# A hybrid decoder layer on one core: two products taken in turn, a DMA turn in the attention, and three shifts of order

## The chip, the core and the metric

The kernel runs on one core of a Trainium2 chip. Its engines work side by side, each through its own queue in order: TensorE (PE, whose weight loads are listed as PEld), VectorE (DVE), ScalarE (ACT), GpSimd (POOL), and SyncE (SP), which here only issues DMAs. The metric is the device time of one execution in microseconds (us); smaller is better. Three executions of the kernel before took 2025.03 us in the median (2021.9 to 2025.69).

## What is computed

One decoder layer for 256 tokens of width 2048, in float32. Cut to what the change touches:

```python
hn = rmsnorm(h, norm_mix_w)
q, k, v, g_ret, xr, yr, g_a, g_b = split(hn @ w_in)
ret = head_groupnorm(chunkwise_retention(rotary(q), rotary(k), v), ret_gn_w)
ret_out = silu(g_ret) * ret
rnn_out = gelu(yr) * rg_lru(causal_dwconv(xr))
merged = sigmoid(g_a) * (ret_out @ w_proj_ret) + sigmoid(g_b) * (rnn_out @ w_proj_rnn)
h = h + merged @ w_mix_out
...
logits = einsum("bshd,bmhd->bhsm", q, k) * 512 ** -0.5     # 4 heads, 256 memory tokens
p = softmax(logits)
o = einsum("bhsm,bmhd->bshd", p, v)
h = h + o @ xa_w_o
h = h + conv_gated_ffn(rmsnorm(h, norm_ffn_w))
return rmsnorm(h, final_norm_w)
```

## The kernel before

**Products.** All weights are laid out in DRAM in the order in which they are used (`weight_stream`, L110), in chunks of four k-tiles: 512 rows by 512 columns of float32, 1 MB. A product of 256 tokens with a 2048 x 512 block of weights is four chunks. To reach nearly float32 accuracy, both operands are split into a high part and a rest, and three matmuls replace one (`products_n`, L340: high x high, low x high, high x low). A chunk is so 24 matmuls of 128 x 128 by 512.

**Supply of weights.** `prefetch` (L228) issues a chunk's load on SP's queue into one of 3 `raw` buffers; ScalarE copies it to `hi` (L269) and VectorE subtracts to get `lo` (L270), each for two k-tiles at a time, into 6 buffers of two k-tiles, which is three chunks. `chunks` (L284) runs the prefetch two chunks ahead of the chunk that is multiplied. A `raw` buffer is free for the next load when its `lo` is done; a `hi` or `lo` buffer when TensorE has used it.

**Work between chunks.** After each chunk a counter goes up by one; `later(n, fn)` (L280) emits `fn` after n + 1 further chunks. The order of the matmuls on TensorE is the order in which they are written. On the other engines a planner orders the instructions: of those that it takes to be ready, the one that was written first goes first, apart from a few with high priority (the copies of `by_dma`, the scaling in `turned_rows`).

**Turning.** A product gives rows by token; the next one needs them by feature. `by_dma` (L372) does it: ScalarE copies the 16-bit halves of the rows to two `planes` (L380), SP issues two transposing DMAs (L382), and after `wait` + 1 chunks two ScalarE copies (L391) join the halves to `f`. `split_pair` (L416) or `split_cols` (L442) then makes the high and low operands.

**Around the change.** `retain` (L603) runs four heads of the retention at a time; after the last head `normalise` (L640) scales the eight half-rows of the four heads by VectorE (L648) and ScalarE (L653) and turns them in two pieces; the results, `words`, are first used some 60 chunks later. `gated` (L799) makes a block of the merge; block 3 of `merged` is the last thing before the product with `w_mix_out`, whose chunk k needs block k of `merged`. `residual` (L828) runs the four blocks of that product and, later, of the one with `xa_w_o`: each block's sum is added to the residual rows (L835), squared (L850), and turned. `memory_steps` (L854) adds, ahead of block 1, eight squarings of the memory's rows (L488). The eight 512 KB loads of x and of the memory (L824 and L825) stand on SP's queue just ahead of that product. In the cross attention a product for k and one for q alternate for four heads; `softmax` (L874) makes the probabilities, `transpose_probs` (L896) turns them by four TensorE transposes (L209) and a ScalarE copy (L906); `attend` (L925) multiplies them with v, one chunk after v's product.

At the start two products run in turn already, in chunks of 2, 2, 4, 4 and 4 k-tiles, fed by loads of x by feature (`xt`, L525). The rows of x by token (`nat`, L223) are only needed for the sum of squares that scales the first results; their four loads are issued on ScalarE's queue.

Of the kernel before, what the change touches and what calls it, by code (L numbers as in the profile page):

```python
# [106 lines left out]
    return [(sum(sizes[:j]), n) for j, n in enumerate(sizes)]  # L107


def weight_stream():  # L110

    out = [
        [(w, row + k * P, n, c) for k, n in pieces(i, nk)]
        for i, (w, row, nk, c) in enumerate(weight_plan())
    ]
    out[:2] = [[one for pair in zip(*out[:2]) for one in pair]]
    out[-4:-1] = [[c for o in out[-4:-1] for c in o[:-1]] + [o[-1] for o in out[-4:-1]]]
    return [one for chunks in out for one in chunks]


# [10 lines left out]
def hybrid_layer(  # L131
# [73 lines left out]
    def mm(*a, **k):  # L205
        tc.keep_in_program_order(pe.matmul(*a, **k))  # L206

    def turn_small(*a):
        tc.keep_in_program_order(pe.transpose(*a))  # L209


    plan = weight_plan()
    stream = weight_stream()
# [4 lines left out]
    def load_x(n):  # L218
        while len(xin) < n:
            t = big([P, 2, BW], s="nat")  # L220
            rows = x[0].rearrange("(t p) d -> p t d", p=P)
            c = len(xin) * BW
            act.dma_start(out=t, in_=rows[:, :, c : c + BW])  # L223
            xin.append(t)

    at = [0]
# [1 line left out]
    def prefetch(n):  # L228
        while len(ahead) < n and taken[0] < len(stream):
            i = taken[0]  # L230
            name, row, nk, c = stream[i]
            taken[0] += 1
            size = nk * P * BW
            src = wall[at[0] : at[0] + size].rearrange("(p k n) -> p k n", p=P, k=nk)
            at[0] += size
            raw = wp.tile([P, KC, BW], F32, tag="raw", bufs=RAW_BUFS, name=nm("raw"))
            k2 = row // (KH * P)
            early = i < 2 * len(EARLY)
            own = early and i % 2 == 0
            cuts = range(nk + 1) if i < 2 else range(0, nk + 1, KH) if i < 6 else (0, nk)  # L240
            if own:
                xs.load(k2 + 1)
            for a, b in zip(cuts, cuts[1:]):
                sp.dma_start(out=raw[:, a:b, :], in_=src[:, a:b, :])  # L244
                if i == 0 and a == 0:
                    sp.dma_start(out=xs.rest[0], in_=xs.rest[1])
                elif own and a == 0:
                    xs.load(k2 + nk // KH)
            if i == 7:
                sp.dma_start(out=cid, in_=consts[:, 0:C_DEC])  # L250
                sp.dma_start(out=pa[:, 16:P], in_=by_feature[:, 16:P])
                sp.dma_start(out=pb, in_=by_feature[:, P : P + 80])
            if i == 11:
                sp.dma_start(out=pf.rearrange("p a n -> p (a n)"), in_=by_feature[:, P + 80 :])
            if i in (8, 9):
                for b in (2 * i - 16, 2 * i - 15):
                    sum_squares(xin[b], ss0, b, pin=True)
            parts = []
            for k in range(0, nk, KH):
                if own:  # L260
                    xs[k2 + k // KH]
                hi = wp.tile([P, KH, BW], F32R, tag="hi", bufs=PART_BUFS, name=nm("hi"))
                lo = wp.tile([P, KH, BW], F32R, tag="lo", bufs=PART_BUFS, name=nm("lo"))
                for cs in (slice(k, k + 1), slice(k + 1, k + 2)) if i < 2 else (slice(k, k + KH),):
                    ds = slice(cs.start - k, cs.stop - k)
                    if i == 0:
                        dve.tensor_copy(hi[:, ds], raw[:, cs, :])  # L267
                    else:
                        act.copy(hi[:, ds], raw[:, cs, :])  # L269
                    dve.tensor_tensor(  # L270
                        out=lo[:, ds], in0=raw[:, cs, :], in1=hi[:, ds].bitcast(F32), op=ALU.subtract
                    )
                parts.append((hi, lo))
            ahead.append(((row, c), parts))
            if i >= 4:
                load_x(min(4, i - 3))

    pending, step = [], [0]

# [323 lines left out]
    def retain(g, qr, kr, vs, dec, gates):  # L603
# [34 lines left out]
                normalise()  # L638

        def normalise():  # L640
            rows = [big([P, 2, BW], s="rows") for _ in range(2)]
            rstd = rsqrt_small(stats[:, :, 1], 8, 1.0, GN_EPS).rearrange("p (h t) -> p h t", t=2)
            for tt in range(2):
                dve.tensor_scalar_mul(rstd[:, :, tt], rstd[:, :, tt], rs0[:, tt : tt + 1])
            for hh in range(4):
                for tt in range(2):
                    y = raws[hh][:, tt, :]
                    dve.scalar_tensor_tensor(  # L648
                        out=y, in0=y, scalar=stats[:, 2 * hh + tt, 0:1],
                        in1=gates[hh // 2][:, tt, (hh % 2) * DV : (hh % 2 + 1) * DV],  # L650
                        op0=ALU.subtract, op1=ALU.mult,
                    )
                    act.mul(rows[hh // 2][:, tt, (hh % 2) * DV : (hh % 2 + 1) * DV], y, rstd[:, hh, tt : tt + 1])  # L653
            for i, r in enumerate(rows):
                by_dma(r, words.append, 2 + i)

        for hh in range(4):
            later(hh, lambda hh=hh: scores(hh))
# [159 lines left out]
    for b in range(4):  # L818
        m = gated(O_GA, "w_proj_ret", ret, b, big([P, 2, BW], s="m"))
        dve.tensor_add(m, m, mb[b])  # L820
        by_dma(m, turn_merged)


    hrow = [load_rows(x, c) for c in range(4)]  # L824
# [3 lines left out]
    def residual(w, st, out, wcol, steps=None):  # L828

        ss = sums()  # L830
        for b in range(4):
            if steps:
                steps(b)
            h = hrow[b]
            dve.tensor_add(h, h, gemm_n(w, 0, st, NT, b * BW))  # L835
            squares(h, ss, b)
            by_dma(hrow[b], lambda f, b=b: turn(f, b, out, wcol))
        return ss
# [30 lines left out]
    lscale = sp_.tile([P, 2], F32, tag="ls", name="lscale")  # L869
    dve.tensor_scalar_mul(lscale, rstd_rows(ss1), float(XD**-0.5))  # L870

    pTs, done = [], [0]

    def softmax(q, k):  # L874
        lg = small()
        for tt in range(2):
            for i in range(4):
# [4 lines left out]
        mx, nb, sm, rsm = (sp_.tile([P, 2], F32, tag=f"sx{i}", name=nm("sx")) for i in range(4))  # L882
        dve.tensor_reduce(out=mx, in_=lg, axis=AX.X, op=ALU.max)
        dve.scalar_tensor_tensor(out=nb, in0=mx, scalar=-1.0, in1=lscale, op0=ALU.mult, op1=ALU.mult)
        pr_ = tmp("prob")
        for tt in range(2):
            c1 = slice(tt, tt + 1)
            act.activation(
# [2 lines left out]
        dve.reciprocal(rsm, sm)  # L891
        for tt in range(2):
            dve.tensor_scalar_mul(pr_[:, tt, :], pr_[:, tt, :], rsm[:, tt : tt + 1])
        later(1, lambda: transpose_probs(pr_))

    def transpose_probs(pr_):  # L896
        t = small()
        for kt in range(2):
            for tt in range(2):
                turn_small(t[:, kt, tt * P : (tt + 1) * P], pr_[:, tt, kt * P : (kt + 1) * P], ident)  # L900
        if done[0] == len(pTs):
            two = tp.tile([P, 2, BW], F32, tag="sig", bufs=2, name=nm("pT"))
            pTs.extend(two[:, i, :].rearrange("p (k s) -> p k s", s=S) for i in range(2))
        pT = pTs[done[0]]
        done[0] += 1
        act.copy(pT, t)  # L906

    def split_block(f):
        return [split_pair(f[:, 2 * pr : 2 * pr + 2, :]) for pr in range(2)]
# [1 line left out]
    def key_query(b):  # L911
# [2 lines left out]

        def query(f):
            qs = split_block(f)
            later(1, lambda: softmax(qs, ks))

        turned_rows(gemm_n("xa_w_q", 0, h1s, NT, b * BW), None, query)

# [19 lines left out]

    for b in range(XH):
        v = split_rows(gemm_n("xa_w_v", 0, ms, NT, b * BW), rsms[0])
        later(0, lambda b=b, v=v: attend(b, v))

    h2s = []
    ss2 = residual("xa_w_o", osp, h2s, p_ffn)
# [153 lines left out]
```

## Time and profile before

| what | before |
|---|---|
| median of the runs (lowest, highest) | 2025.03 us (2021.9, 2025.69) |
| the profiled execution: time, and span from its first to its last instruction | 2022.28 us, 2020.5 us |
| mean granted TensorE clock | 0.996 |
| VectorE busy, ScalarE busy | 1264.3 us, 1246.0 us |
| DMA: moved, mean rate | 421.99 MB, 209 GB/s |

How to read the lines further down: in a chain of waits or a timeline the first number is the start in us from the first instruction, the second the time taken; `x24` counts instructions that were merged into one row; `[4.04 <-ACT s L423]` says that the engine idled 4.04 us before and what ended it. In groups of instructions, `busy, mean ns` is followed by the idle time ahead of the group's instructions. In a table of windows each engine has its busy us and the number of instructions that touch the window; then follow the granted clock, the DMA engines' busy share and the rate.

### The profile page before, as it was taken

What the parts mean: (1) busy time and instruction counts of PE and PEld (TensorE: products, weight loads), DVE (VectorE), ACT (ScalarE), POOL (GpSimd) and SP (SyncE); (2) the same over time, 40 slices, a digit from 0 to 9 for tenths busy, and PEclk for the clock granted to TensorE, in tenths of its full rate; (3) what the DMA queues carried; (4) which work ended last, traced back from release to release, by engine and by line L of the source; (5) the groups of instructions that cost most, each with busy time, mean ns of one, the idle gap of its engine ahead of it and who ended that gap; (6) DMA issues with size and microseconds to landing.
All of it is one profiled execution on the core that took longest, in us unless ns stands there. A gap on an engine that the chain in (4) does not pass through costs nothing.

```text
span 2020.5 us, 23630 instructions
## 1 busy us (share of the span) xinstructions
PE 2002.3 (99%) x9060; PEld 1666.2 (82%) x9060; DVE 1264.3 (63%) x1563; ACT 1246.0 (62%) x1502; POOL 7.7 (0%) x12
## 2 busy tenths in 40 slices
PE   9999999999999999999999999999999999999998
PEld 7888888888888888788888888888888888888887
DVE  5856756888645555456555554567675577664675
ACT  6546547989434555478666556666774566644763
POOL 0000000000000000000000000000000000000000
PEclk9999999999999999999999999999999999999999
DMA  8665656665555566777766546667666566655663
GB/s 304 225 210 173 234 199 192 228 213 188 208 188 190 197 204 214 259 225 242 219 198 204 182 167 208 209 189 218 228 203 232 193 195 214 227 215 198 210 228 125
DMA packets 185153, 421.99 MB, mean 209 GB/s; under 512 B 127440, under 2 KB 132176, under 8 KB 139984
## 3 DMA queue, kind: packets, MB, share of 16 engines
q1 hardware_dynamic: 183520, 417.85, 62.2%
q10 hardware_dynamic: 1520, 2.63, 0.4%
q8 instruction: 71, 1.16, 0.2%
q14 instruction: 42, 0.34, 0.1%
HBM read 388.46 MB, written 2.10 MB: 193 GB/s over the span
## 4 chain that ended last, share of the span: by engine, by line
PE 97%; ACT 1%; DVE 1%; DMA 1%; issue 1%; SPq 0%; POOL 0%; POOLq 0%; DVEq 0%; ACTq 0%
PE acc L206 94%; PE sm L206 3%; DMA raw<-in_wall 1%; DVE lo L270 0%; ACT f L391 0%; DVE xr L765 0%; ACT pl L380 0%; ACT rows L653 0%; ACT hi L269 0%; POOL ro L507 0%; PE sm L209 0%; SPq L244 0%; DVE s L447 0%; ACT nat L1034 0%; DVE rows L404 0%
## 5 line engine op out<-in xcount | busy, mean ns | idle before, releaser
L206 PE MATMUL acc<-hi,s 128*128 128x512 f32 (+1 forms) x5680 | 1741.6, 388 | 4.2 <-ACT s L423 4.0
L270 DVE TENSOR_TENSOR lo<-raw,hi 128x1024 fp32r<-128x1024 f32 (+1 forms) x714 | 861.1, 1220 | 662.4 <-ACT hi L269 636.5
L206 PEld LDWEIGHTS acc<-hi,s 128*128 128x128 f32 x5680 | 1062.5, 188 | 222.1 <-ACT s L423 4.5
L206 PE MATMUL acc<-lo,s 128*128 128x512 f32 (+1 forms) x2840 | 1100.8, 388 | 2.0 <-DVE lo L270 2.0
L269 ACT CAST hi<-raw 128x1024 fp32r<-128x1024 f32 (+1 forms) x712 | 736.0, 1051 | 535.4 <-PE acc L206 466.7
L206 PEld LDWEIGHTS acc<-lo,s 128*128 128x128 f32 x2840 | 533.7, 188 | 111.6 <-DVE lo L270 2.7
L391 ACT COPY f<-pt 128x1024 uint16<-128x1024 uint16 x114 | 146.5, 1350 | 68.8 <-DMA pt<-pl 68.6
L380 ACT COPY pl<-rows 128x1024 uint16<-128x1024 uint16 x90 | 89.8, 1046 | 66.1 <-DVE rows L404 58.2
L404 DVE TENSOR_SCALAR rows<-acc,ro 128x512 f32<-128x512 f32 x68 | 47.8, 747 | 2.4 <-PE acc L206 2.4
L957 DVE SCALAR_TENSOR_TENSOR fv<-f,pf,fv 128x255 f32<-128x255 f32 (+1 forms) x88 | 35.8, 479 | 0.7 <-ACT fv L955 0.7
L957 DVE SCALAR_TENSOR_TENSOR fg<-f,pf,fg 128x255 f32<-128x255 f32 (+1 forms) x88 | 35.6, 478 | 0.0
L955 ACT ACTIVATE fv<-f,pf 128x256 f32<-128x256 f32 x44 | 22.9, 596 | 0.0
L955 ACT ACTIVATE fg<-f,pf 128x256 f32<-128x256 f32 x44 | 22.9, 594 | 0.0
L423 ACT ACTIVATE s<-fo 128x512 fp32r<-128x512 f32 x22 | 13.6, 635 | 14.1 <-DVE fo L977 14.1
L380 ACT COPY pl<-nat 128x1024 uint16<-128x1024 uint16 x16 | 16.0, 1046 | 9.6 <-DVE nat L835 9.6
L765 DVE SCALAR_TENSOR_TENSOR xr<-f,pa,xr 128x255 f32<-128x255 f32 (+2 forms) x48 | 20.1, 481 | 2.1 <-ACT xr L763 2.0
L446 ACT ACTIVATE s<-f,pb 128x256 fp32r<-128x256 f32 x48 | 20.4, 501 | 0.0
L447 DVE SCALAR_TENSOR_TENSOR s<-f,pb,s 128x256 fp32r<-128x256 f32 x48 | 19.9, 480 | 0.0
L206 PEld LDWEIGHTS sm<-s,s 128*128 128x128 f32 x144 | 18.8, 191 | 0.9
L206 PE MATMUL acc<-s,hi 128*128 128x512 f32 x64 | 17.6, 413 | 1.0 <-DVE hi L267 1.0
L206 PE MATMUL sm<-s,s 128*128 128x256 f32 (+1 forms) x144 | 18.6, 279 | 0.0
L421 DVE TENSOR_TENSOR s<-f,s 128x512 fp32r<-128x512 f32 x16 | 10.3, 687 | 10.0 <-ACT s L420 10.0
(154 smaller groups left out, 630.0 us busy)
## 6 DMA issues: line engine op xcount, KB each, us to landing
raw<-in_wall SPq DMA_DIRECT2D x352, 1024.0 KB, 4.9
raw<-in_wall SPq DMA_DIRECT2D x6, 512.0 KB, 6.4
nat<-in_x ACTq DMA_DIRECT2D x4, 512.0 KB, 8.2
nat<-in_x SPq DMA_DIRECT2D x4, 512.0 KB, 5.7
nat<-in_mem SPq DMA_DIRECT2D x4, 512.0 KB, 9.0
xt<-in_mem_t SPq DMA_DIRECT2D x8, 256.0 KB, 3.7
pt<-pl SPq DMA_TRANSPOSE x114, 4.9
xt<-in_x_t SPq DMA_DIRECT2D x7, 256.0 KB, 6.3
```

Source lines behind the costliest of these rows:

```text
L206: tc.keep_in_program_order(pe.matmul(*a, **k))
L269: act.copy(hi[:, ds], raw[:, cs, :])
L270: dve.tensor_tensor(out=lo[:, ds], in0=raw[:, cs, :], in1=hi[:, ds].bitcast(F32), op=ALU.subtract)
L380: act.copy(planes[:, :, h, :], words[:, h])
L391: act.copy(halves_[:, h], turned_[:, h])
L404: dve.tensor_scalar_mul(rows[:, tt, :], a[:, tt, :], r[:, tt : tt + 1])
L423: act.mul(t[:, :, 0:S], src, scale)
L446: act.activation(t[:, j, 0:S], src[:, j, :], AF.Identity, scale=wcol(j))
L447: dve.scalar_tensor_tensor(out=t[:, j, S:BW], in0=src[:, j, :], scalar=wcol(j), in1=t[:, j, 0:S].bitcast(F32), op0=ALU.mult, op1=ALU.subtract,
L765: dve.scalar_tensor_tensor(out=y[:, s:S], in0=z[:, 0 : S - s], scalar=p_cw(3 - s, t), in1=y[:, s:S], op0=ALU.mult, op1=ALU.add,)
L955: act.activation(y, z[:, j, :], AF.Identity, scale=pf[:, 2, t : t + 1], bias=pf[:, 3, t : t + 1])
L957: dve.scalar_tensor_tensor(out=y[:, s:S], in0=z[:, j, 0 : S - s], scalar=pf[:, 2 - s, t : t + 1], in1=y[:, s:S], op0=ALU.mult, op1=ALU.add,)
```

## The change

- `weight_stream` lays the first two blocks of `w_mix_out`, and the first two of `xa_w_o`, in turn: three chunks of block 0, three of block 1, then the last chunk of each. `residual` runs the matmuls in that order. The last block of `merged` is joined at wait 3 in place of 1.
- `softmax` writes the probabilities of two heads into one `big` tile, which `by_dma` turns; the four TensorE transposes per head and the copy out of PSUM are gone. `attend` runs two chunks after v's product in place of one.
- In `normalise` the scaling by ScalarE and the turn are emitted one chunk later for heads 0 and 1 and two chunks later for heads 2 and 3; their join comes at wait 4 in place of 2 and 3.
- The loads of x by token move from ScalarE's queue to SP's, one prefetch step later and ahead of that step's copies. Three loads of constants move from step 7 to 8, one from 11 to 13.

```diff
--- before.py
+++ after.py
@@ -107,6 +107,11 @@
     return [(sum(sizes[:j]), n) for j, n in enumerate(sizes)]
 
 
+def in_turn(products):
+
+    return [c for o in products for c in o[:-1]] + [o[-1] for o in products]
+
+
 def weight_stream():
 
     out = [
@@ -114,7 +119,10 @@
         for i, (w, row, nk, c) in enumerate(weight_plan())
     ]
     out[:2] = [[one for pair in zip(*out[:2]) for one in pair]]
-    out[-4:-1] = [[c for o in out[-4:-1] for c in o[:-1]] + [o[-1] for o in out[-4:-1]]]
+    out[-4:-1] = [in_turn(out[-4:-1])]
+    for w in ("w_mix_out", "xa_w_o"):
+        i = [c[0][0] for c in out].index(w)
+        out[i : i + 2] = [in_turn(out[i : i + 2])]
     return [one for chunks in out for one in chunks]
 
 
@@ -205,9 +213,6 @@
     def mm(*a, **k):
         tc.keep_in_program_order(pe.matmul(*a, **k))
 
-    def turn_small(*a):
-        tc.keep_in_program_order(pe.transpose(*a))
-
 
     plan = weight_plan()
     stream = weight_stream()
@@ -220,7 +225,7 @@
             t = big([P, 2, BW], s="nat")
             rows = x[0].rearrange("(t p) d -> p t d", p=P)
             c = len(xin) * BW
-            act.dma_start(out=t, in_=rows[:, :, c : c + BW])
+            sp.dma_start(out=t, in_=rows[:, :, c : c + BW])
             xin.append(t)
 
     at = [0]
@@ -246,11 +251,13 @@
                     sp.dma_start(out=xs.rest[0], in_=xs.rest[1])
                 elif own and a == 0:
                     xs.load(k2 + nk // KH)
-            if i == 7:
+            if i >= 5:
+                load_x(min(4, i - 4))
+            if i == 8:
                 sp.dma_start(out=cid, in_=consts[:, 0:C_DEC])
                 sp.dma_start(out=pa[:, 16:P], in_=by_feature[:, 16:P])
                 sp.dma_start(out=pb, in_=by_feature[:, P : P + 80])
-            if i == 11:
+            if i == 13:
                 sp.dma_start(out=pf.rearrange("p a n -> p (a n)"), in_=by_feature[:, P + 80 :])
             if i in (8, 9):
                 for b in (2 * i - 16, 2 * i - 15):
@@ -272,8 +279,6 @@
                     )
                 parts.append((hi, lo))
             ahead.append(((row, c), parts))
-            if i >= 4:
-                load_x(min(4, i - 3))
 
     pending, step = [], [0]
 
@@ -638,7 +643,6 @@
                 normalise()
 
         def normalise():
-            rows = [big([P, 2, BW], s="rows") for _ in range(2)]
             rstd = rsqrt_small(stats[:, :, 1], 8, 1.0, GN_EPS).rearrange("p (h t) -> p h t", t=2)
             for tt in range(2):
                 dve.tensor_scalar_mul(rstd[:, :, tt], rstd[:, :, tt], rs0[:, tt : tt + 1])
@@ -650,9 +654,17 @@
                         in1=gates[hh // 2][:, tt, (hh % 2) * DV : (hh % 2 + 1) * DV],
                         op0=ALU.subtract, op1=ALU.mult,
                     )
-                    act.mul(rows[hh // 2][:, tt, (hh % 2) * DV : (hh % 2 + 1) * DV], y, rstd[:, hh, tt : tt + 1])
-            for i, r in enumerate(rows):
-                by_dma(r, words.append, 2 + i)
+
+            def two_heads(i):
+                rows = big([P, 2, BW], s="rows")
+                for hh in (2 * i, 2 * i + 1):
+                    for tt in range(2):
+                        c = (hh % 2) * DV
+                        act.mul(rows[:, tt, c : c + DV], raws[hh][:, tt, :], rstd[:, hh, tt : tt + 1])
+                by_dma(rows, words.append, 4)
+
+            for i in range(2):
+                later(i, lambda i=i: two_heads(i))
 
         for hh in range(4):
             later(hh, lambda hh=hh: scores(hh))
@@ -818,7 +830,7 @@
     for b in range(4):
         m = gated(O_GA, "w_proj_ret", ret, b, big([P, 2, BW], s="m"))
         dve.tensor_add(m, m, mb[b])
-        by_dma(m, turn_merged)
+        by_dma(m, turn_merged, 1 if b < 3 else 3)
 
 
     hrow = [load_rows(x, c) for c in range(4)]
@@ -828,11 +840,16 @@
     def residual(w, st, out, wcol, steps=None):
 
         ss = sums()
+        products = [steps_n(w, 0, st, NT, b * BW) for b in range(4)]
         for b in range(4):
             if steps:
                 steps(b)
+            if b == 0:
+                for one in products[:2]:
+                    for _ in range(NT // KC - 1):
+                        next(one)
             h = hrow[b]
-            dve.tensor_add(h, h, gemm_n(w, 0, st, NT, b * BW))
+            dve.tensor_add(h, h, ended(products[b]))
             squares(h, ss, b)
             by_dma(hrow[b], lambda f, b=b: turn(f, b, out, wcol))
         return ss
@@ -869,9 +886,9 @@
     lscale = sp_.tile([P, 2], F32, tag="ls", name="lscale")
     dve.tensor_scalar_mul(lscale, rstd_rows(ss1), float(XD**-0.5))
 
-    pTs, done = [], [0]
-
-    def softmax(q, k):
+    pTs, probs = [], []
+
+    def softmax(b, q, k):
         lg = small()
         for tt in range(2):
             for i in range(4):
@@ -882,7 +899,9 @@
         mx, nb, sm, rsm = (sp_.tile([P, 2], F32, tag=f"sx{i}", name=nm("sx")) for i in range(4))
         dve.tensor_reduce(out=mx, in_=lg, axis=AX.X, op=ALU.max)
         dve.scalar_tensor_tensor(out=nb, in0=mx, scalar=-1.0, in1=lscale, op0=ALU.mult, op1=ALU.mult)
-        pr_ = tmp("prob")
+        if b % 2 == 0:
+            probs.append(big([P, 2, BW], s="prob"))
+        pr_ = probs[-1][:, :, (b % 2) * S : (b % 2 + 1) * S]
         for tt in range(2):
             c1 = slice(tt, tt + 1)
             act.activation(
@@ -891,19 +910,8 @@
         dve.reciprocal(rsm, sm)
         for tt in range(2):
             dve.tensor_scalar_mul(pr_[:, tt, :], pr_[:, tt, :], rsm[:, tt : tt + 1])
-        later(1, lambda: transpose_probs(pr_))
-
-    def transpose_probs(pr_):
-        t = small()
-        for kt in range(2):
-            for tt in range(2):
-                turn_small(t[:, kt, tt * P : (tt + 1) * P], pr_[:, tt, kt * P : (kt + 1) * P], ident)
-        if done[0] == len(pTs):
-            two = tp.tile([P, 2, BW], F32, tag="sig", bufs=2, name=nm("pT"))
-            pTs.extend(two[:, i, :].rearrange("p (k s) -> p k s", s=S) for i in range(2))
-        pT = pTs[done[0]]
-        done[0] += 1
-        act.copy(pT, t)
+        if b % 2 == 1:
+            by_dma(probs[-1], lambda f: pTs.extend(f[:, 2 * i : 2 * i + 2, :] for i in range(2)))
 
     def split_block(f):
         return [split_pair(f[:, 2 * pr : 2 * pr + 2, :]) for pr in range(2)]
@@ -914,7 +922,7 @@
 
         def query(f):
             qs = split_block(f)
-            later(1, lambda: softmax(qs, ks))
+            later(1, lambda: softmax(b, qs, ks))
 
         turned_rows(gemm_n("xa_w_q", 0, h1s, NT, b * BW), None, query)
 
@@ -940,7 +948,7 @@
 
     for b in range(XH):
         v = split_rows(gemm_n("xa_w_v", 0, ms, NT, b * BW), rsms[0])
-        later(0, lambda b=b, v=v: attend(b, v))
+        later(1, lambda b=b, v=v: attend(b, v))
 
     h2s = []
     ss2 = residual("xa_w_o", osp, h2s, p_ffn)
```

## The prediction

> **What bounds the kernel now.** I read the page first: shares, chain, groups.
>
> ```profile
> span 2020.5 us, 23630 instructions
> PE 2002.3 (99%) x9060; PEld 1666.2 (82%) x9060; DVE 1264.3 (63%) x1563; ACT 1246.0 (62%) x1502; POOL 7.7 (0%) x12
> PE 97%; ACT 1%; DVE 1%; DMA 1%; issue 1%; SPq 0%; POOL 0%; POOLq 0%; DVEq 0%; ACTq 0%
> ```
>
> TensorE bounds it: 97% of the chain. Only three things can give time: matmuls left out, stalls of TensorE filled, matmuls at a slower clock. So the second view is who TensorE waited for, and the third the chain in order of time, where the stalls stand.
>
> ```profile
> PE acc L206 <- ACT s L423: 4.0, 1, 4.0
> PE acc L206 <- DVE lo L270: 3.9, 5, 2.0
> ```
>
> ```profile
> 494.14 347.96 PE acc L206 x1535
> ...
> 846.35 84.08 PE acc L206 x359
> ...
> 988.34 10.91 PE acc L206 x48
> 999.24 0.44 PE sm L209 x4
> ```
>
> Over its whole length the kernel waits 8 us, in six places. Between them it is a clean stream: 347.96 us for 1535 matmuls is 0.227 us each, and two chunks of 24 take 10.91, so a chunk 5.45. One wait of 4.0 is for a split by ScalarE (L423); of the five for weights the longest are 2.0 and 1.4.
>
> The big one is the last chunk of block 0 of the product with `w_mix_out`. Its timeline on TensorE, and the windows around it:
>
> ```profile
> 846.35 1.52 PE L206 MATMUL acc<-hi,s 128*128 128x512 f32 x2 [4.04 <-ACT s L423]
> ```
>
> ```profile
> 846.30:850.90 4.60, 4.55 (x10) 3.35 (x11) 1.29 (x2) 0.52 (x1) 0.00 (x0) 0.50 1.06 412
> 841.92:851.33 9.41, 5.37 (x13) 3.64 (x12) 3.71 (x4) 4.61 (x5) 0.00 (x0) 0.64 1.06 408
> ```
>
> The second window begins and ends at a matmul's start and holds 12 starts (13 less the one already running). Twelve at 0.227 are 2.72 us; it took 9.41. So the stall costs **6.7 us**: 4.2 of waiting, and 2.5 because the clock granted afterwards was 0.50 for ten matmuls. The reader should see that a stall can cost more than its wait.
>
> Why was the split late? ScalarE's timeline and the transposes:
>
> ```profile
> 842.17 1.05 ACT L269 CAST hi<-raw 128x1024 fp32r<-128x1024 f32 x1 [0.32 <-PE acc L206]
> 843.12 2.51 ACT L391 COPY f<-pt 128x1024 uint16<-128x1024 uint16 x2
> 845.67 1.15 ACT L423 ACTIVATE s<-f 128x512 fp32r<-128x512 f32 x2
> ```
>
> ```profile
> 832.85 2.62 SPq L382 DMA_TRANSPOSE pt<-pl  x2
> pt<-pl SPq DMA_TRANSPOSE x2, 3.2
> ```
>
> The second transpose was issued by about 834.2 and landed 3.2 later, near 837.4. But the join (L391) stood in ScalarE's queue behind a cast that waited for TensorE to free a buffer, at 842.1. TensorE had by then nothing left that it could multiply.
>
> **The change part by part.**
>
> *Blocks 0 and 1 of the mix-out in turn.* Block 0's last chunk is now the seventh rather than the fourth: three chunks, 16.3 us, more to do before it. The second split ended at 846.8; with its rest on VectorE behind it, I count 848. The chunk would now start at 842.1 + 16.3 = 858.4. The join's wait of 3 has it emitted after the fifth chunk, still ahead of its use. Gain **6.7**.
>
> What is late next? First, the weights: without the stall TensorE wants them 6.7 us sooner, right behind 4 MB of x and memory rows. The load behind those:
>
> ```profile
> 840.12 17.74 SPq L244 DMA_DIRECT2D raw<-in_wall  x4
> raw<-in_wall SPq DMA_DIRECT2D x1, 1024.0 KB, 12.1
> ```
>
> The first of those four was issued at 840.1 and landed 12.1 later, at 852.2. Casts run three chunks ahead of use, so it serves the chunk at 858.4: casts of 2.1 and one `lo` of 1.2 leave 3 us. Hidden; it costs nothing.
>
> Second, ScalarE. Block 0's tail now comes one chunk before block 1's, in place of four, and the eight squarings of the memory stand between them. Groups of ScalarE during the mix-out, and VectorE's `lo`:
>
> ```profile
> L269 ACT CAST hi<-raw 128x1024 fp32r<-128x1024 f32 x29 | 29.9, 1050 | 21.5 <-PE acc L206 15.5 <-issue 6.0
> L391 ACT COPY f<-pt 128x1024 uint16<-128x1024 uint16 x8 | 10.2, 1337 | 1.7 <-DMA pt<-pl 1.7
> L380 ACT COPY pl<-nat 128x1024 uint16<-128x1024 uint16 x6 | 6.0, 1046 | 3.4 <-DVE nat L835 3.4
> L488 ACT ACTIVATE junk<-nat 128x512 f32<-128x512 f32 x8 | 4.9, 619 | 0.0
> L850 ACT ACTIVATE junk<-nat 128x512 f32<-128x512 f32 x6 | 3.7, 623 | 0.0
> L446 ACT ACTIVATE s<-f,pb 128x256 fp32r<-128x256 f32 x8 | 3.4, 499 | 0.0
> L270 DVE TENSOR_TENSOR lo<-raw,hi 128x1024 fp32r<-128x1024 f32 (+1 forms) x714 | 861.1, 1220 | 662.4 <-ACT hi L269 636.5 <-PE acc L206 10.4
> ```
>
> A block's tail is planes 2.0, squares 1.2, join 2.5, operands 1.7. Count from the end of block 0. Planes end at about 4.2, squares at 5.4, the memory's squarings (written before the next casts) 4.9 later with block 1's planes (2.0) among them: 12.3. Now the casts for the fourth chunk from there, which TensorE starts at 16.3. If block 0's join and operands and block 1's squares go ahead of them (5.4), the first cast ends at 18.7 and its `lo` at 19.9: a stall of 3.6. If the join goes behind, `lo` is ready at 15.8, and a chunk later at 22.0 against 21.8: 0.2. Between 0.2 and 3.6 I take **2.0**, the middle, as no row shows which comes first.
>
> *`xa_w_o` in turn.* No stall stands there now, so nothing is won. ScalarE has the same two tails, but no memory squarings: by the same count the casts are done at 7, and the next at 17 against 21.8. Cost nothing; it would be 0.2 to 3.6 as above if other work stood there.
>
> *The heads' rows.* The stall of 2.0:
>
> ```profile
> 337.71 0.61 PE L206 MATMUL acc<-hi,s 128*128 128x512 f32 x2
> 340.31 0.50 PE L206 MATMUL acc<-lo,s 128*128 128x512 f32 x1 [1.98 <-DVE lo L270]
> 340.65 0.62 PE L206 MATMUL acc<-hi,s 128*128 128x512 f32 x2
> ```
>
> ```profile
> 319.42 2.12 ACT L653 ACTIVATE rows<-rc,ro 128x256 f32<-128x256 f32 x5 [4.07 <-DVE ro L644]
> ```
>
> Three matmuls took 2.94 where 0.68 is due: 2.26 lost, at the full clock. ScalarE stood blocked for 4.07 on the scaling's factors with casts queued behind it. Emitted a chunk later, the scaling finds its factors ready; ScalarE does the same work with 4.07 more room, against 2.26 needed. The joins move three chunks on, to about 346, where ScalarE is busy too, but with the room just won. Gain **2.3**; at worst 0.
>
> *The probabilities.* Four TensorE transposes per head take 0.44, so four heads
>
> ```profile
> L209 PE MATMUL sm<-cid,prob 128*128 128x128 f32 x16 | 2.4, 272 | 0.0
> L906 ACT COPY pT<-sm 128x512 f32<-128x512 f32 x4 | 2.3, 576 | 0.0
> L269 ACT CAST hi<-raw 128x1024 fp32r<-128x1024 f32 x62 | 65.0, 1055 | 54.0 <-PE acc L206 53.9
> ```
>
> give **1.75**. In return ScalarE gets four plane copies and four join copies (4.0 + 5.1 by the groups above) for 2.3 of copies: 7 us more over 180, where it idles 54 us ahead of casts because TensorE is not yet done with the buffers (third row). Hidden. The joins wait on ScalarE for the transposes, casts behind them:
>
> ```profile
> ACT f L391 <- DMA pt<-pl: 68.6, 31, 4.0
> ```
>
> 31 such waits of at most 4.0 stall TensorE nowhere now; two more cost nothing under a lead of two chunks. SP gets four transposes, 5.2 us of issue in all, with weight loads behind them; this is a rival below. Attending a chunk later uses nothing sooner than before.
>
> *Start.* The four loads of x move to SP's queue, ahead of some loads of weights there. The chain's last load of weights at the start, and TensorE's last wait there:
>
> ```profile
> 11.35 6.72 DMA raw<-in_wall
> ```
>
> ```profile
> 20.51 2.45 PE L206 MATMUL acc<-s,lo 128*128 128x256 f32 x14 [1.42 <-DVE lo L270]
> ```
>
> That load is under way from 11.35 to 18.1. If x went ahead of it, 0.52 MB at the 404 to 412 GB/s of the window above is 1.3 us each, 2.6 for two; if not, at best the 1.4 goes. I take 0, in -1.4 to +2.6. From then to 337 TensorE waited for nothing, so later shifts of loads are covered.
>
> Sum: -6.7 + 2.0 - 2.3 - 1.75 = -8.7 on the profiled execution's 2022.28 (span and 1.8 around it): 2013.5. That execution lies at the low end of the runs, 2.75 under their median; I add half, 1.4: **2015**.
>
> [...]
>
> **Rivals.**
>
> 1. *The mix-out's tails cost their most and the clock drops too.* 3.6 + 2.5 in place of 2.0: 4.1 more, **2019**. For it: the order in which work was written. Against: a wait of 3.6 lies between 1.98 and 4.04, and no row shows which way.
> 2. *The heads' stall stays*: the joins or the next convolution hold the casts up as before. **2017.3**. For it: ScalarE is nearly full there. Against: the 4.07 blocked.
> 3. *The change does not do what it says in the mix-out*: the join is again placed behind a cast that waits for the very chunk before it. The 6.7 stays: **2021.7**. Against: three more chunks.
> 4. *Slower: SP's queue in the cross attention.* SP stops at a transpose until its planes are written, with the weight loads behind:
>
> ```profile
> SPq L382 <- ACT hi L269: 135.3, 41, 9.2
> raw<-in_wall SPq DMA_DIRECT2D x352, 1024.0 KB, 4.9
> ```
>
> The probabilities' planes hang on a long chain (logits, maximum, exponential, sum, scaling). If SP is held as long as the longest here, 9.2, then load 4.9, cast 1.1 and `lo` 1.2 make 16.4; weights are two chunks ahead, 10.9; TensorE stalls 5.5, and 2.5 more at the slow clock: 8.0, twice 16: **2031**. It decides from a hold of 3.7 on. Against: holds up to 9.2 have stalled nothing so far, since loaded `raw` buffers cover too.
>
> **How the numbers follow.** Forecast 0.60 (its own range 2010 to 2018), rival 1 0.12, rival 2 0.10, rival 3 0.10, rival 4 0.08. A measurement of this kernel tells 0.2%, 4 us, from no change: faster ends at 2021.0, slower begins at 2029.1. Forecast and rivals 1 and 2 are faster, less 0.02 for their upper edge: 0.80; rival 3 and that edge 0.12; rival 4 0.08. Low end: full gain of 10.7 and 1.4 at the start from 2022.28, less the offset: 2010, with a margin of 1. High end: rival 3, 2022. So 2009 to 2022 leaves out rival 4 and little else.
>
> **What would show it.** Right: no TensorE wait for L423 in the mix-out and no granted 0.50 after the start; no wait near 338; no row L209; matmuls still 0.227. The squares' place: a TensorE wait for `lo` of 0.2 to 3.6 some three chunks after block 0's end. Wrong: a wait for L423 still there; a wait for `lo` between 985 and 1145; waits before 20 us longer than now.

## The result, and the profile after

| | before | after |
|---|---|---|
| median of five runs in the same session (lowest, highest) | 2022.33 us (2021.9, 2025.69) | 2013.99 us (2013.28, 2016.63) |
| the profiled execution: time, span, granted clock | 2022.28, 2020.5, 0.996 | 2016.58, 2014.5, 0.997 |

The ratio of the times is 0.9959, with a 95% interval of 0.9948 to 0.997: 8.3 us less, between 6.1 and 10.5. The forecast was 2015. Two executions further down ran at a granted clock of 0.65 and 0.85 (2884.99 us with the heads' rows alone, 2218.03 with the squarings earlier); the medians and ratios leave them out.

The page of the kernel after, its span, its engines, and the shares of the chain that ended last:

```profile
span 2014.5 us, 23604 instructions
PE 1999.1 (99%) x9044; PEld 1664.3 (83%) x9044; DVE 1263.5 (63%) x1563; ACT 1247.8 (62%) x1506; POOL 7.7 (0%) x12
PE 96%; DMA 1%; ACT 1%; issue 1%; DVE 1%; SPq 0%; POOLq 0%; POOL 0%; ACTq 0%; DVEq 0%
```

TensorE still bounds it, with the 16 transposes gone (9044 matmuls for 9060). What TensorE waited for longest:

```profile
PE acc L214 <- DVE lo L277: 3.3, 5, 1.4
PE acc L214 <- ACT hi L276: 2.5, 1, 2.5
```

The 4.0 for the split (L423 before, L428 now) is gone. A wait of 2.5 for a weights' cast has come.

**Where the old stall stood**, ScalarE's timeline:

```profile
839.67 1.05 ACT L276 CAST hi<-raw 128x1024 fp32r<-128x1024 f32 x1 [0.32 <-PE acc L214]
840.63 2.56 ACT L396 COPY f<-pt 128x1024 uint16<-128x1024 uint16 x2
843.22 1.15 ACT L428 ACTIVATE s<-f 128x512 fp32r<-128x512 f32 x2
851.06 2.00 ACT L276 CAST hi<-raw 128x1024 fp32r<-128x1024 f32 x2 [6.69 <-DMA raw<-in_wall]
```

The join still runs behind casts, at 840.6, but its result is used 16 us later. ScalarE then idles 6.69 us for the load behind the 4 MB of rows, and TensorE, which has three chunks in hand, does not notice.

**Where the new stall stands**, TensorE first, then ScalarE from the end of block 0 on:

```profile
877.50 0.39 PE L214 MATMUL acc<-lo,s 128*128 128x512 f32 x1
880.37 0.73 PE L214 MATMUL acc<-hi,s 128*128 128x512 f32 x2 [2.48 <-ACT hi L276]
881.63 0.79 PE L214 MATMUL acc<-lo,s 128*128 128x512 f32 x1 [0.53 <-DVE lo L277]
882.22 1.05 PE L214 MATMUL acc<-hi,s 128*128 128x512 f32 x2
```

```profile
861.37 1.06 ACT L276 CAST hi<-raw 128x1024 fp32r<-128x1024 f32 x1 [0.30 <-PE acc L214]
863.49 1.99 ACT L385 COPY pl<-nat 128x1024 uint16<-128x1024 uint16 x2 [1.06 <-DVE nat L852]
865.39 0.63 ACT L867 ACTIVATE junk<-nat 128x512 f32<-128x512 f32 x1
...
866.63 0.62 ACT L493 ACTIVATE junk<-nat 128x512 f32<-128x512 f32 x1
...
872.14 2.55 ACT L396 COPY f<-pt 128x1024 uint16<-128x1024 uint16 x2 [0.51 <-DMA pt<-pl]
...
876.38 1.98 ACT L385 COPY pl<-nat 128x1024 uint16<-128x1024 uint16 x2
...
879.29 3.87 ACT L276 CAST hi<-raw 128x1024 fp32r<-128x1024 f32 x4
```

For 16.9 us, from 862.4 to 879.3, ScalarE casts no weights. It does block 0's planes and squares, the memory's eight squarings (4.9 us of it), block 0's join and operands, block 1's planes and squares: all of it was written ahead of the next cast. That cast could have run sooner. TensorE ran dry at 877.7; two chunks of 5.45 earlier, at 866.8, it had freed the last of the cast's buffers, and the load had landed at 861.8. TensorE uses up its three chunks, waits 2.48 and 0.53, and then runs six matmuls at 0.427 us. From 877.50 to 884.78 are ten matmuls, due 2.27 and taking 7.28: **5.0 lost** of the 6.7 won.

**The heads' rows**, ScalarE in the stretch where it used to stand for 4.07, and TensorE where it waited at 338:

```profile
323.11 1.70 ACT L663 ACTIVATE rows<-rc,ro 128x256 f32<-128x256 f32 x4
```

```profile
338.62 0.39 PE L214 MATMUL acc<-lo,s 128*128 128x512 f32 x1
338.84 0.62 PE L214 MATMUL acc<-hi,s 128*128 128x512 f32 x2
```

The scaling finds its factors ready, and TensorE's matmuls are 0.227 apart. For the first four heads, at 181.7, it still stands for 4.35 (4.08 in before); TensorE waits for nothing there in either kernel, so such a stand is not a stall by itself.

**The cross attention**, SP's waits at transposes between 970 and 1170 us:

```profile
SPq L387 <- ACT hi L276: 22.0, 6, 6.5
SPq L387 <- ACT v L440: 7.0, 1, 7.0
```

The holds of 6.5 and 7.0 are those ahead of the probabilities' transposes, issued from 1035.3 and from 1128.1. SP is held up to 7.0, and TensorE waits for nothing from 940 to 1290. One small wait is new further on, at 1303 in the first chunks behind the product with `xa_w_o`:

```profile
1303.11 0.39 PE L214 MATMUL acc<-hi,s 128*128 128x512 f32 x1
1303.98 0.50 PE L214 MATMUL acc<-hi,s 128*128 128x512 f32 x1 [0.48 <-DVE s L452]
```

### The profile page after: what moved, and what is told of

Read it like the earlier page. It is cut to its first block, busy times and chain, and to the rows that moved or that the text cites. A ratio compares the mean times of both kernels' runs of the same rounds, so it can differ in the third digit from the quotient of the medians.

```text
span 2014.5 us, 23604 instructions
## 1 busy us (share of the span) xinstructions
PE 1999.1 (99%) x9044; PEld 1664.3 (83%) x9044; DVE 1263.5 (63%) x1563; ACT 1247.8 (62%) x1506; POOL 7.7 (0%) x12
## 4 chain that ended last, share of the span: by engine, by line
PE 96%; DMA 1%; ACT 1%; issue 1%; DVE 1%; SPq 0%; POOLq 0%; POOL 0%; ACTq 0%; DVEq 0%
PE acc L214 94%; PE sm L214 3%; DMA raw<-in_wall 1%; DMA pt<-pl 1%; DVE lo L277 0%; ACT pl L385 0%; ACT hi L276 0%; ACT f L396 0%; ACT junk L867 0%; DVE nat L852 0%; ACT s L451 0%; SPq L249 0%; ACT nat L1042 0%; DVE s L452 0%; SPq L387 0%
## 5 line engine op out<-in xcount | busy, mean ns | idle before, releaser
L396 ACT COPY f<-pt 128x1024 uint16<-128x1024 uint16 x118 | 151.4, 1349 | 85.0 <-DMA pt<-pl 85.0
L428 ACT ACTIVATE s<-fo 128x512 fp32r<-128x512 f32 x22 | 13.6, 633 | 14.2 <-DVE fo L985 14.2
L440 ACT ACTIVATE v<-acc,ro 128x512 fp32r<-128x512 f32 x16 | 10.9, 683 | 7.7 <-DVE v L441 7.7
```

What stands on the lines that cost most here:

```text
L396: act.copy(halves_[:, h], turned_[:, h])
L428: act.mul(t[:, :, 0:S], src, scale)
```

## The experiments

One execution's stages say more than its total here, since the total scatters by 3 us and more. This table is worked out from starts of matmuls in each profiled execution: "start" ends where the first results' scale is spread by matmuls (`sm<-diag`, 49.5 us in before); "heads" at the first matmul with the gates' weights (`rgw`, 344 us in before); "mix-out" runs from the last of these, 149.7 later in every kernel, to the first logits; "rest" from there to the last matmul. Behind that lies a tail of 8.0 to 8.3. In us:

```
                        start   heads  mix-out    rest    span
before                  49.51  294.56   491.54  1026.94  2020.5
after                   49.28  292.29   489.46  1025.77  2014.5
mix-out in turn alone   48.29  296.12   489.56  1027.79  2019.7
heads alone             48.03  292.29   492.39  1026.94  2017.6
probabilities alone     48.68  296.13   491.70  1025.98  2020.2
x loads alone           48.42  294.53   491.09  1027.43  2019.4
before, join pinned     47.99  296.14   492.22  1028.38  2022.7
after, w_o plain        47.58  292.29   491.11  1025.34  2014.1
after again             47.55  292.29   489.38  1025.50  2012.4
after, squarings early  49.76  292.29   486.06  1026.09  2011.9
 ... and on VectorE     48.76  292.29   485.76  1025.74  2010.3
 ... and memory early   48.40  292.29   484.39  1026.25  2009.1
```

### The mix-out in turn, alone

The kernel before with this one part:

```diff
+    i = [c[0][0] for c in out].index("w_mix_out")
+    out[i : i + 2] = [[c for o in out[i : i + 2] for c in o[:-1]] + [o[-1] for o in out[i : i + 2]]]
...
+            if b == 0 and w == "w_mix_out":
+                for one in products[:2]:
+                    for _ in range(NT // KC - 1):
+                        next(one)
...
-        by_dma(m, turn_merged)
+        by_dma(m, turn_merged, 1 if b < 3 else 3)
```

> The kernel before with the first two blocks of the mix-out product in turn and the last block of merged joined at wait 3; nothing else changed. Theory A (the filled stall is given back on ScalarE): the wait for L423 at 842 and its slow clock (6.7 us) are gone, and a new wait for a weight copy comes about 13 us after block 0's end, behind both tails and the memory's squarings, worth 5.0 us with its slow clock as in the changed kernel; net -1.7 us, so within 2 us of the kernel before, and the wait near 338 (2.26 us) is still there. Rival B (the new wait in the changed kernel comes from the other edits, which shifted SP's queue or the weights): no new wait here, net -6.7 us.

Measured: 2020.89, ratio 0.9996 (0.9986 to 1.0005). The wait for the split is gone, and this stands in its place on TensorE:

```profile
880.34 0.39 PE L208 MATMUL acc<-lo,s 128*128 128x512 f32 x1
883.13 0.73 PE L208 MATMUL acc<-hi,s 128*128 128x512 f32 x2 [2.40 <-ACT hi L271]
884.39 0.51 PE L208 MATMUL acc<-lo,s 128*128 128x512 f32 x1 [0.53 <-DVE lo L272]
884.73 0.64 PE L208 MATMUL acc<-hi,s 128*128 128x512 f32 x2
```

The same stall as in the changed kernel, without the slow clock behind it: from 880.34 to 884.73 are four matmuls, due 0.91 and taking 4.39, so 3.5 lost. It begins, as in the changed kernel, 14.0 us behind the start of block 0's planes (866.33 here), which is 16 behind block 0's end and not the 13 that was expected. So it comes from this part and no other. The whole product gains 2.0 by the table (491.54 to 489.56), a third of the 6.7 that the old stall cost. That is less than 6.7 - 3.5 = 3.2, because a wait for operands of the memory costs 1.6 here, where before loses 0.4 at 930:

```profile
934.27 1.02 PE L208 MATMUL acc<-hi,s 128*128 128x512 f32 x2 [1.03 <-ACT s L448]
```

### The heads' rows alone

The kernel before with the changed `normalise` (the part of the diff from `two_heads` on).

> The kernel before with only the scaling and turning of the heads' rows emitted later. Theory A: the wait near 338 goes, -2.3 us; the stall at 842 stays and starts 2.3 us sooner. Rival: the wait only moves to where the joins now stand, between 340 and 400, and the time does not change.

Measured: 2020.19, ratio 0.9988 (0.9979 to 0.9998). The stage to the gates' weights takes 292.29, as in every kernel with this edit. Without it the stage takes 294.5 in two executions and 296.1 in three; these two rows each, of the mix-out alone and of the x loads alone, are why:

```profile
339.06 0.55 PE L208 MATMUL acc<-lo,s 128*128 128x512 f32 x1 [1.95 <-DVE lo L272]
339.41 1.05 PE L208 MATMUL acc<-hi,s 128*128 128x512 f32 x2
```

```profile
339.18 0.50 PE L206 MATMUL acc<-lo,s 128*128 128x512 f32 x1 [1.94 <-DVE lo L272]
339.52 0.63 PE L206 MATMUL acc<-hi,s 128*128 128x512 f32 x2
```

The same wait is followed by a pair of matmuls that takes 1.05 in one execution and 0.63 in the other. So the edit is worth 2.3 or 3.8, in the mean of the five executions 3.2. The edit moves the scaling and the joins together; which of the two shifts did it, this run does not separate.

### The probabilities alone

The kernel before with `softmax` writing two heads into one tile, `by_dma` for it, and `later(1, ...)` for `attend`.

> The kernel before with only the probabilities turned by DMA and each head attended a chunk later. Theory A: the 16 TensorE transposes go, -1.75 us, and TensorE waits for nothing new between 985 and 1215. Rival: SP's queue, held by the transposes, makes a wait for weights there, and the gain is less than 1 us or a loss.

Measured: 2021.96, ratio 0.9998 (0.9989 to 1.0007). The transposes are gone, and no wait stands between 985 and 1215. One does behind the product with `xa_w_o`, though this kernel takes its blocks one after the other:

```profile
1308.60 0.40 PE L206 MATMUL acc<-hi,s 128*128 128x512 f32 x1
1309.67 0.51 PE L206 MATMUL acc<-hi,s 128*128 128x512 f32 x1 [0.67 <-DVE s L447]
1310.01 0.40 PE L206 MATMUL acc<-lo,s 128*128 128x512 f32 x1
```

Two matmuls, due 0.45, took 1.41: 0.96 of the 1.75 is lost again. A single pair of executions would put the gain at 1.0 (1026.94 to 1025.98). But the same wait stands in kernels without this part too: with the x loads alone, 0.53 and 0.34 us pass from one matmul's start to the next at 1308, where 0.227 is due. Over the seven executions with the part the rest takes 1025.8 in the mean, over the five without it 1027.5: the gain is 1.7.

### The loads of x alone

```diff
-            act.dma_start(out=t, in_=rows[:, :, c : c + BW])
+            sp.dma_start(out=t, in_=rows[:, :, c : c + BW])
...
+            if i >= 5:
+                load_x(min(4, i - 4))
```

and the two shifts of the constants.

> The kernel before with one part of the change: the four loads of x by token go out on SP's queue, a prefetch step later, and three loads of constants with them. Theory A (costs and gives nothing: loads of weights in front cover it): the first 50 us look as before but for the scatter of the start, which was 47.6 to 49.8 us from the first instruction to the end of the start in all kernels so far, whether x stood on the one queue or the other; time 2022, ratio 0.998 to 1.002. Rival B (x goes ahead of a load of weights and makes the product wait): the start takes 51 us or more and the time is 2.6 more, 2025. Rival C (ScalarE freed of issuing four loads helps): TensorE's last wait at the start, 1.4, is gone and the time is 2020.5.

Measured: 2022.15, ratio 1.0 (0.9991 to 1.0009). The start took 48.42, and TensorE's last wait there is the one of before:

```profile
20.98 1.94 PE L206 MATMUL acc<-s,lo 128*128 128x256 f32 x14 [1.44 <-DVE lo L272]
```

Over all executions the start takes 48.5 in the mean with x on the one queue (five) and on the other (seven). It scatters from 48.0 to 49.5 on the one and from 47.6 to 49.8 on the other.

### The join first, in the kernel before

If the old stall came from the join's place behind a cast, one edge in the order of instructions should remove it without taking blocks in turn. Here the first cast that is written after the last join of `merged` is kept behind it on ScalarE:

```diff
+                        cast = act.copy(hi[:, ds], raw[:, cs, :])
+                        if pin_cast:
+                            tc.keep_in_program_order(cast)
+                            pin_cast.clear()
...
+        if len(merged) == 8:
+            pin_cast.append(True)
```

> The kernel before, its products in the old order, with one edge added: the first weight copy written after the last block of merged is joined may not go ahead of that join and its split on ScalarE. Theory A (the join's place in ScalarE's queue made the stall): the join runs at about 837.5, when the transposes have landed, the split is ready at about 841.5, and the stall of 6.7 us is gone or below 1 us without any product taken in turn; no crowd behind block 0 either; net -6 to -6.7 us. Rival B (the operand is late by its own chain, and only more chunks ahead of it help): the wait for L423 stays above 3 us.

Measured: 2021.72, ratio 0.9999 (0.999 to 1.0008). ScalarE, and TensorE further on:

```profile
837.47 2.57 ACT L395 COPY f<-pt 128x1024 uint16<-128x1024 uint16 x2 [3.61 <-DMA pt<-pl]
...
853.66 2.00 ACT L270 CAST hi<-raw 128x1024 fp32r<-128x1024 f32 x2 [8.65 <-DMA raw<-in_wall]
...
860.28 0.62 ACT L492 ACTIVATE junk<-nat 128x512 f32<-128x512 f32 x1
...
865.18 1.98 ACT L270 CAST hi<-raw 128x1024 fp32r<-128x1024 f32 x2
```

```profile
866.26 0.73 PE L206 MATMUL acc<-hi,s 128*128 128x512 f32 x2 [2.11 <-ACT hi L270]
...
928.39 0.50 PE L206 MATMUL acc<-hi,s 128*128 128x512 f32 x1 [0.96 <-ACT s L450]
930.18 0.79 PE L206 MATMUL acc<-hi,s 128*128 128x512 f32 x1 [1.28 <-DVE s L451]
...
931.20 1.05 PE L206 MATMUL acc<-hi,s 128*128 128x512 f32 x2
```

The cause of the old stall is confirmed: the join starts at 837.5, and the wait for the split is gone. The expected gain is not there. TensorE reaches the weights behind the 4 MB sooner, but the load lands no sooner (its cast starts at 853.7, behind a wait of 8.65 for it), the squarings then hold the next cast until 865.2, and two stalls take the time back: 3.2 lost at 864, and 4.4 at 927, on operands of the memory, where before loses 0.4. In the second, six matmuls at 0.427 us, where 0.227 is due, follow waits of only 0.96 and 1.28. In before the same two casts start at almost the same times, 852.9 and 864.5, but behind the old stall TensorE comes too late to wait for them.

### The changed kernel with the memory's squarings earlier

In the changed kernel `steps(1)` is called behind the six chunks in turn, ahead of the seventh, so that the squarings are ready in ScalarE's idle time behind the 4 MB:

```diff
-            if steps:
+            if steps and b != 1:
                 steps(b)
...
+                if steps:
+                    steps(1)
```

> The changed kernel with the memory's eight squarings written ahead of the seventh chunk of the mix-out, where ScalarE idles, in place of between block 0's tail and block 1's. Theory A (the squarings crowd ScalarE's queue behind block 0): the wait for a weight copy at 877 us (2.6 us, with what follows 3.5 to 5.0) is gone or below 0.5 us; 3 to 5 us less than the changed kernel. Rival (two tails one chunk apart are enough to crowd it, or the weights' loads are late): the wait stays above 2 us.

Measured: 2012.52, ratio 0.9951 (0.9934 to 0.9967). TensorE's longest waits, and ScalarE's cast that came at 879.29 in the changed kernel, with block 0's join:

```profile
PE acc L214 <- DVE lo L277: 3.0, 5, 1.4
PE acc L214 <- DVE s L452: 2.0, 2, 1.3
```

```profile
867.20 1.99 ACT L276 CAST hi<-raw 128x1024 fp32r<-128x1024 f32 x2
...
872.65 2.56 ACT L396 COPY f<-pt 128x1024 uint16<-128x1024 uint16 x2
```

No cast is waited for, and the mix-out falls from 489.46 to 486.06. So the squarings at their old place were what made the new stall. They take 4.9 us but delayed the cast by 12.1: without them it finds ScalarE free at 867.2 and goes ahead of the join, as nothing written earlier is ready then; behind them the join and both blocks' tails, written ahead of it, were ready and went first. A wait of 1.3 for operands of the memory, at 922, is left.

### The product with `xa_w_o` not in turn

```diff
-    for w in ("w_mix_out", "xa_w_o"):
+    for w in ("w_mix_out",):
```

> The changed kernel with the blocks of the output product in their old order. Theory A (the wait of 0.75 us near 1303 is the last block's own chain of turn, join and split, at the edge of its time whichever way blocks 0 and 1 run; the run with the probabilities alone had it too): the wait is still between 0 and 1 us at the fourth chunk of the feed-forward product, and the time is within 0.5 us of the changed kernel. Rival (taking blocks 0 and 1 in turn made it): it is gone, -0.75 us.

Measured: 2016.09, ratio 0.9968 (0.9955 to 0.998), where the changed kernel, run again on the same chip, had 0.9961 (0.9946 to 0.9976): no difference that can be told, though intervals this wide allow one of 1.5 us. The rest takes 1025.34 here and 1025.50 there, and the small wait at 1303 is still there (0.3 lost, 0.5 in the changed kernel run again). No cost or gain of this part shows.

### The changed kernel again

No edit.

> The changed kernel once more, beside its variants on one chip. Median near 2014 us. Theory A (whether TensorE's clock drops after a wait of 2 to 3 us differs from one execution to the next): the wait near 877 is again 2.5 to 2.9 us, with or without matmuls of 0.43 us behind it, and the two give times 1 to 3 us apart. Rival (it drops whenever the wait is as long as here): the slow matmuls follow again.

Measured: 2014.63, ratio 0.9961 (0.9946 to 0.9976). The stall at 876, on TensorE:

```profile
878.10 0.73 PE L214 MATMUL acc<-hi,s 128*128 128x512 f32 x2 [1.95 <-ACT hi L276]
...
880.53 1.05 PE L214 MATMUL acc<-hi,s 128*128 128x512 f32 x2
```

The slow clock came again, here behind waits of 1.95 and 0.53; the stall lost 4.6 us, and 6.2 in the execution with `xa_w_o` plain. Of the four executions with this stall (after, after again, `xa_w_o` plain, the mix-out alone) only the last kept the full clock, and so did the pinned join behind its 2.11 and 0.53. What decides it, these runs do not tell.

### The squarings early and on VectorE

The same early place, with the squarings as `scalar_tensor_tensor` on VectorE, which is busy 83.2 us of the 142 between 842 and 984 in the changed kernel, ScalarE 102.9:

```diff
-                sum_squares(mnat[c], ss, c)
+                sum_squares_v(mnat[c], ss, c)
```

> As the run with the squarings early, but done by VectorE. Theory A: the wait at 877 is gone as there; time equal to that run within 1 us, as ScalarE no longer sets the pace of the mix-out. If ScalarE's total work still limited that stage, this one would be 1 to 3 us faster than it. Rival: as there, the wait stays above 2 us.

Measured: 2012.87, ratio 0.9951 (0.9936 to 0.9966), as on ScalarE. The wait for the memory's operands is still there, on TensorE:

```profile
922.17 0.50 PE L214 MATMUL acc<-hi,s 128*128 128x512 f32 x1 [1.07 <-DVE s L452]
```

### And the memory's operands a block earlier

```diff
-        if b == 3:
+        if b == 2:
             ms.load(2)
```

> The changed kernel with the memory's squarings on VectorE and ahead of the seventh chunk (as the run before it, 2012.9), and now the loads and the splits of the memory's first operands begin one block (four chunks) earlier. Theory A (the last wait of the mix-out, 1.3 us near 921 for these operands, was their late emission): that wait is gone, nothing else changes, time 2011.5, 0.6 per 1000 less than the run before it. Rival B (the loads of the memory by feature now delay the weights' loads behind them, or the splits delay the casts of blocks 2 and 3, as the pinned join did): a new wait of 1 us or more between 885 and 925, time 2013 or more.

Measured: 2010.85, ratio 0.9941 (0.9927 to 0.9954). A window from 842 to 984 us of this kernel, and of the changed one, with the busy us and instructions of TensorE, its weight loads, VectorE, ScalarE and GpSimd, the granted clock, the DMA share and the rate:

```profile
842.00:984.00 142.00, 142.00 (x639) 118.05 (x638) 92.40 (x125) 102.54 (x137) 1.39 (x2) 1.00 0.79 255
```

```profile
842.00:984.00 142.00, 138.99 (x617) 114.82 (x616) 83.24 (x102) 102.86 (x145) 1.39 (x2) 0.99 0.77 249
```

TensorE is busy 142.00 of 142.00: no stall is left in the mix-out, which takes 484.39, 7.15 less than in before. This version beats before by 11.9 us (9.3 to 14.8) in the ratio, and its runs (2009.42 to 2011.29) lie below the changed kernel's (2013.28 to 2016.63).

## Why the prediction was right, and where its terms were not

- **TensorE bounds, and only its stalls, its clock and its matmuls give time.** So it was: but for 0.2 us behind the last matmul, what the stages differ by is found in those three. The prediction's 8 us of waits in six places leave out another 2.1 in the first 20 us, where the change was to give nothing.
- **The old stall, -6.7.** The mechanism was as forecast, and the pinned join shows it apart from the rest: the wait goes when the join goes first. The load behind the 4 MB was hidden, as the prediction's count had it (ScalarE waited 6.69 for it, TensorE not).
- **ScalarE's crowd, +2.0: the step that was mis-sized.** The place was right (a wait for a cast of weights, three chunks behind block 0's end, 14.0 us behind the start of its planes, where the count has 14.1: 16.3 less the 2.2 to their start), and so was the cause, as the earlier squarings show. The order was the bound that the prediction put at 3.6 (join, operands and squares ahead of the casts), and 3.5 was lost in the execution that kept the clock. Choosing the middle of 0.2 and 3.6 was the mistake: the planner lets what was written first go first, and it put all of that work ahead of the casts, with ScalarE idle for only 1.06 and 0.51 us in that stretch. The prediction named the order of writing as what speaks for rival 1, and still took the middle because no row showed it. With the slow clock behind it the crowd cost 4.6 to 6.2, 5.0 in the profiled execution, and so the mix-out went as rival 1 had it (6.1 by its count). What the product gained was -2.1, for -4.7 forecast, and the sign "no granted 0.50 after the start" failed with it: the clock was 0.62 from 880.3 to 884.8.
- **The slow clock behind a shorter wait.** The prediction counted no slowing behind a wait of 2, since the row of 1.98 showed none. One row was too little. Behind 1.95 the pair took 1.05 in the mix-out alone and 0.63 behind 1.94 in the x loads alone. In the pinned join slow matmuls stand behind 0.96 and 1.28, and none behind 2.11 and 0.53. So the length of the waits does not tell it alone; what else does was not shown.
- **The heads' rows, -2.3.** Right by the one execution it was worked out from, and the edit alone takes the stall away. That the scaling's stand of 4.07 made it is likely but not shown apart from the later joins. In the mean it was 3.2, since the slow clock came along in three of five.
- **The probabilities, -1.75.** 1.7 in the mean. SP was held up to 7.0, and nothing came of it: rival 4 fell. Its deciding hold of 3.7 was too low; a likely reason is that it left out the loaded `raw` buffers, which the prediction named only as what speaks against it. Rivals 2 and 3 fell too: no wait stands near 338, and none is for the split.
- **`xa_w_o` in turn, and the start, 0 each.** Both were 0.
- **The 1.4 added at the end** rested on three runs of before. With 31 and with 15 more its median came out at 2022.29 and 2021.96, close to the profiled execution, so it should have been 0. It stood against part of the crowd's error, and the heads' extra 0.9 against another: that 2015 came so close was partly luck, as errors of both signs met. With the measured means it would read 2022.3 - 3.2 - 1.8 - 1.7 - 0.2 (the tail behind the last matmul) = 2015.4; the mix-out's 1.8 is the mean of four executions with the part against that of four without.

Open: the parts run alone sum, by their ratios, to some 3.6 us (0.8 + 2.4 + 0.4 + 0), the whole to 8.3. Each ratio's interval is about 2 us to either side, so the two sums just about meet; the stages account for 6.9. That the slow clock falls more often in one kernel than in another could make up the rest, but it was not tried.

## What to carry to other kernels

A stall is also time in which the other engines and queues catch up: before counting its removal as a gain, follow the next loads and casts at the earlier times, as the pinned join shows (4.0 of wait removed, nothing won). Where a product's tails move closer together, write out the crowded engine's queue instruction by instruction in the order in which it was written; work with a far due date (here eight squarings) belongs in a hole of that engine, not between two tails. And where one execution scatters by as much as the effect, compare stages over several executions, not totals of two.

## What the runs showed of the hardware

- Near 339 us a wait of TensorE of 1.94 to 1.95 us was followed by about eight matmuls at 0.427 in place of 0.227 us in three executions (granted clock 0.79 from 338 to 346), and by none in one (1.00); before's own, of 1.98, by none (1.00). In the pinned join two waits of 0.96 and 1.28, with one matmul between them, were followed by six such matmuls. The stall near 339 so cost 2.3 or 3.8, and this alone made 1.6 us of scatter between executions of the same code.
- The start scatters by 2.2 us (47.55 to 49.76) over executions of the same code there. Here too some executions have slow matmuls behind the waits at 17 to 20 us and others none: behind a wait of 1.44 fourteen matmuls of 256 columns took 2.62 in after and 1.94 with the x loads alone. The windows from 20 to 50 us of after and of after again (the granted clock is the third number from the end):

```profile
20.00:50.00 30.00, 29.73 (x148) 25.62 (x149) 16.56 (x28) 18.50 (x37) 0.70 (x1) 0.94 0.80 311
```

```profile
20.00:50.00 30.00, 29.88 (x155) 25.74 (x156) 18.20 (x31) 20.25 (x39) 0.71 (x1) 1.00 0.82 314
```

In the same 30 us, 148 matmuls against 155.
